# Gathering the 32-column work of a decoder step into fewer slots: when the modulation weights are asked for, and how many of their steps run together

## The chip, the core and the metric

The kernel runs on one core of a Trainium2 chip. The metric is the time of one execution in device microseconds, lower being better. Three timed runs of the kernel before lie between 1823.52 and 1826.77 us, with a median of 1824.22 us.

## The reference

One decoder layer over 256 prompt tokens and 8 sample tokens, in float32. A modulation vector is made from a conditioning input, three mixers run in parallel and are merged, and a squared-ReLU MLP follows:

```python
mod = jax.nn.silu(c) @ p['w_ada'][l] + p['b_ada'][l]
sh1, sc1, gt1, sh2, sc2, gt2 = jnp.split(mod[:, None, :], 6, axis=-1)
h = rmsnorm(x, p['g_pre_mix'][l]) * (1.0 + sc1) + sh1
z = h @ p['w_in'][l]
...
y_a = spatial_gating(...)                                  # branch A
o_hg, S_hg = gated_linear_recurrence(q_hg, k_hg, ...)      # branch B, 8 heads
o_g, S_g = gated_linear_recurrence(q_g, k_g, ...)          # branch C, 4 heads
merged = gates[:, :, 0] * (branches[0] @ p['w_branch'][l, 0])
...
x = x + gt1 * rmsnorm(merged @ p['w_out'][l], p['g_post_mix'][l])
h2 = rmsnorm(x, p['g_pre_mlp'][l]) * (1.0 + sc2) + sh2
y2 = jnp.square(jax.nn.relu(h2 @ p['w_mlp_up'][l])) @ p['w_mlp_down'][l]
x = x + gt2 * rmsnorm(y2, p['g_post_mlp'][l])
```

The samples carry states: for each of 8 sample tokens, the recurrences B and C read a state from memory, decay it, add an outer product, write it back and read it with the query.

## The kernel before

All 264 tokens stand in the columns of the moving operand and the weights are stationary. The unit of the large products is a **granule**: 512 KB of a weight matrix, that is four blocks of 128 rows by 256 columns. Each weight tile `raw` is split on the chip into a rounded high part `whi` (a cast on ScalarE, line 109) and a rest `wlo` (a subtraction on VectorE, line 106), and a granule is 24 matmuls of 128x264: `whi` with both halves of the activations and `wlo` with the first (lines 659 to 661). The loads of `raw` go through SyncE's queue, four buffers deep; `Stream.ahead` keeps two granules split ahead of TensorE. Granules are counted here from the start of the program.

Beside the large products stand small ones whose stationary operand has only 32 columns, so that four of them share the array:

- the **modulation steps**: `mod` is built 2048 columns at a time (a round), in 16 steps of 1 MB of `w_ada`. A step is four matmuls at line 376 (eight in the trace, since each is run as two). `Rounds.load` asks for its two half-tiles of 512 KB; the first step of a batch goes into `araw`, the others into tiles `b` of the common pool. `Rounds.tick` decides when, `Rounds.due` whether a batch can be run. Four rounds of 16 steps run beside the mixers and the MLP; the first two of the six parts of `mod` are made earlier, by other code (line 308).
- the **levels** (line 679): 32x32 products of the recurrences within a chunk.
- the **samples** (line 686): the queries of a sample token against its updated state `st`. A state is fetched by a DMA from GpSimd's queue, scaled on ScalarE (line 1104), given the outer product with `vbc` on VectorE (line 1106), and written back, again by GpSimd's queue. `vbc` holds value rows, repeated over the partitions by a DMA; there are two buffers of `vbc`.

`slot()` runs whatever of the three kinds waits, one after the other. `background()` is called once per granule: it advances the clock `now`, pumps the generators of the mixers, and calls `slot()` by a rule: when a batch of modulation steps is due and either a level or sample has waited or `pace` granules have passed since the last load, or when a level or sample has waited four granules.

What sets the order: TensorE's and GpSimd's instructions stand as the code is written. ScalarE's, VectorE's and SyncE's are placed by a scheduler in this part of the program, and each engine then runs its own list in order. The recurrence B runs in two groups of heads (first and second group below), C is the third group.

Of the kernel before, what the change touches and what calls it, by code (L numbers as in the profile page):

```python
# [48 lines left out]
SLOT_WAIT = 4  # L49
# [2 lines left out]
FETCHED = 3  # L52
AGE = 2
ADA_LAND = 4


@with_exitstack
def hybrid_step_kernel(
# [27 lines left out]
    def blk(shape=None, dt=F32):  # L86
        shape = shape or [P, 4, NT]
        return blkp.tile(shape, dt, tag="b", name=nm("b"))

    def sm(shape=None):  # L90
        return psm.tile(shape or [P, 512], F32, tag="sm", name=nm("sm"))
# [230 lines left out]
    class Rounds:  # L322
# [2 lines left out]

        def __init__(self):
            self.todo, self.ws, self.done, self.at = [], [], None, 0
            self.pace, self.batch = 5, 1

        def load(self, place=None):  # L330
            r, k = self.todo.pop(0)
# [18 lines left out]
        def due(self):  # L350
            if self.ws:
                return self.full() and now[0] >= self.at + ADA_LAND
            return self.done is not None and not self.todo and now[0] >= self.at + 2 * ADA_LAND

        def tick(self):
            if self.todo and not self.full() and now[0] >= self.at + self.pace:
                self.load()

        def steps(self, n=None):
# [28 lines left out]
    rounds = Rounds()  # L388

    now = [0]  # L390
# [273 lines left out]
    levels, samples = [], []  # L664

    def slot():

        lv = [x for x in levels if x[0] + AGE <= now[0]][:2]
        sv = [x for x in samples if x[0] + AGE <= now[0]]
        del levels[:len(lv)]  # L670
        del samples[:len(sv)]
        if lv:
            pl = sm([P, 2, 8, 32])
            for i, (_, lhs, rhs, _) in enumerate(lv):
                for h in range(4):
                    for hf in range(2):
                        for b in range(4):
                            t0 = hf * P + b * 32
                            T.matmul(pl[32 * b:32 * b + 32, i, 2 * h + hf, :], lhs[:, h, t0:t0 + 32], rhs[:, h, t0:t0 + 32], start=True, stop=True)  # L679
        if sv:  # L680
            G, qm, os_ = sv[0][1]
            nh = 512 // G.dv
            po = sm([P, G.dv])
            for h in range(4):
                for i, (_, _, b, sts) in enumerate(sv):
                    T.matmul(po[32 * h:32 * h + 32, :], qm[:, h, b, :], sts[h // nh][:, h % nh, :], start=i == 0, stop=i == len(sv) - 1)  # L686
        if rounds.due():
            rounds.steps()
        for i, (_, _, _, put) in enumerate(lv):
            put(pl[:, i])  # L690
        if sv:
            if sv[0][2] == 0:
                V.tensor_copy(os_, po)
            else:
                add(os_, os_, po)

    later = []

    def background():

        now[0] += 1
        while later and later[0][0] < now[0]:
            later.pop(0)[1]()
        bg.pump(rate[0])
        bs.pump(rate[1])
        wait = max([now[0] + 1 - AGE - x[0] for x in levels + samples] + [0])
        if wait and any(x[1][0].i == 2 for x in samples):
            wait += 2
        if rounds.due() and (wait or now[0] >= rounds.at + rounds.pace) or wait >= SLOT_WAIT:
            slot()  # L710
        rounds.tick()

# [3 lines left out]
    def linear(w, k0, nk, c0, width, xh, xl):  # L716

        acc = new_acc()
        kc = min(nk, 1024 // width)
        for kb in range(0, nk, kc):  # L720
            granule(w, k0, kc, c0, width, [acc], xh, xl, kb, kb == 0, kb + kc == nk)
            background()
        return acc[:, 0:width // P, 0:NT]
# [4 lines left out]
    def pair(b, g):  # L728
        return b[:, 2 * g:2 * g + 2, :]
# [9 lines left out]
    def zin(c0, width=CW):  # L739
        return linear(win, 0, KT, c0, width, hH, hL)  # L740
# [233 lines left out]
    def log_sigmoid(out, z, a):  # L974

        S.activation(a, z, AF.Abs)
        yield
        S.activation(a, a, AF.Exp, scale=-1.0)
        yield 1.6
        S.activation(a, a, AF.Ln, bias=1.0)  # L980
        yield 1.8
        V.scalar_tensor_tensor(out, z, 0.0, a, ALU.min, ALU.subtract)
        yield
# [45 lines left out]
    def gla_group():  # L1029
        G = Group()  # L1030
        G.dv, G.i = 256, 2
        G.q, G.g, G.k, G.v = blk(), blk(), blk(), [blk(), blk()]
        wl = blk([P, 512 + NT])
        wup, lr = wl[:, 0:512], wl[:, 512:512 + NT]
        nc.gpsimd.memset(wl, 0.0)
        nc.gpsimd.dma_start(wup[0:16], gla_w_up[0])
        for s in range(2):
            z = zin(6144 + s * CW)
            S.copy(pair(G.q, s), z)
        for s in range(2):  # L1040
            z = zin(6656 + s * CW)
            S.activation(pair(G.k, s), z, AF.Copy, scale=GLA_SCALE)
        z = zin(9216, P)
        S.copy(lr[0:16], z[0:16, 0, :])
        for s in range(4):
            z = zin(7168 + s * CW)
            S.copy(pair(G.v[s // 2], s % 2), z)
            ps = sm()
            T.matmul(ps[:, 0:NT], wup[:, s * P:(s + 1) * P], lr, start=True, stop=True)
            V.tensor_scalar(G.g[:, s, :], ps[:, 0:NT], bupT[:, s:s + 1], None, ALU.add)  # L1050
        G.s_in = lambda b, h, n: state_gla[0, b, h:h + n].rearrange("h k v -> k h v")
        G.s_out = lambda b, h, n: gla_sample[0, b, h:h + n].rearrange("h k v -> k h v")
        G.p_out = lambda h, n: gla_prompt[0, 0, h:h + n].rearrange("h k v -> k h v")

        def gates():
            yield from log_sigmoid(G.g, G.g, blk())
            V.tensor_scalar(G.g, G.g, 1.0 / GLA_TAU, None, ALU.mult)
            yield

        G.gates = gates  # L1060
        return G
# [246 lines left out]
    for i in range(2):  # L1308
        Gs.append(hg_group(i))
        gens.append(mixer_r(Gs[i]))  # L1310
        bg.g.append(gens[i])
    rate[:] = RATES[0]
    Gs.append(gla_group())
    gens.append(mixer_r(Gs[2]))
    bg.g.append(gens[2])
# [15 lines left out]
    def branch(n, parts):  # L1331
        for m in range(8):
            if m == 0:
                yh, yl = parts()
            z = zin(9232 + n * D + m * CW)
            gt = tmp([P, 2, NT], "gt")
            S.activation(gt, z, AF.Tanh, scale=0.5)
            pr = linear(w_branch[0, n], 0, 8, m * CW, CW, yh, yl)
            if n == 0 and m % 2 == 0:
                mg[m // 2] = blk()  # L1340
            dst = pair(mg[m // 2], m % 2)

            if n == 0:
                V.scalar_tensor_tensor(dst, gt, 1.0, pr, ALU.add, ALU.mult)
            else:
                V.scalar_tensor_tensor(gt, gt, 1.0, pr, ALU.add, ALU.mult)
                add(dst, dst, gt)
            if n == 2 and m % 2 == 1:
                a, b = blk(dt=F32R), blk(dt=F32R)
                split_tokens(mg[m // 2], a, b)  # L1350
                mh.append(a)
                ml.append(b)

    def gate_tiles(c0):

        out = [blk(), blk()]
        for s in range(4):
            z = zin(c0 + s * CW)
            gt = pair(out[s // 2], s % 2)
            S.activation(gt, z, AF.Tanh, scale=0.5)  # L1360
            V.scalar_tensor_tensor(gt, gt, 1.0, z, ALU.add, ALU.mult)
        return out
# [5 lines left out]
    def parts_b(gates):  # L1368
        for i in range(2):
            finish(i)  # L1370
            o = Gs[i].o[0]
            V.scalar_tensor_tensor(o, o, hgnT, gates[i], ALU.mult, ALU.mult)
        return yparts([Gs[0].o[0], Gs[1].o[0]])
# [16 lines left out]
    rate[:] = RATES[1]  # L1390
    branch(0, parts_a)
    gates_b = gate_tiles(5120)
    rounds.batch = 2
    branch(1, lambda: parts_b(gates_b))
    rate[:] = RATES[2]
    rounds.pace, rounds.batch = 4, 4
    gates_c = gate_tiles(8192)
    rate[:] = RATES[3]
    branch(2, lambda: parts_c(gates_c))
# [90 lines left out]
    rounds = pre  # L1490
# [112 lines left out]
    def begin_up():  # L1603

        accs = [new_acc(), new_acc()]
        for k in range(0, KT, 2):
            granule(w_mlp_up[0], 0, 2, 0, 2 * CW, accs, h2H, h2L, k, k == 0, k + 2 == KT)
            if k % 4 == 0 and k + 4 < KT:
                quad(k // 4 + 1)
            elif k + 6 < KT:  # L1610
                residual(k // 4 + 2)
            elif k + 2 == KT:
                residual(0)
            if k >= 8:
                background()
        return [a[:, :, 0:NT] for a in accs]
# [141 lines left out]
```

## Time and profile before

| | |
|---|---|
| median of three runs | 1824.22 us |
| profiled execution, its time | 1827.14 us |
| its span | 1825.4 us |
| TensorE busy | 1780.2 us (98%) |
| VectorE, ScalarE, GpSimd busy | 1181.2, 1001.2, 132.3 us |
| data moved | 442.05 MB, mean 242 GB/s |
| matmuls of lines 659 to 661 | 3 x 4624 |
| matmul records of line 376 | 296 from `araw`, 216 from `b` |

The profile comes from one execution. Matmuls are pipelined, so a busy TensorE is not TensorE at its peak: what a small product costs is read in the timeline, from the start of the last large matmul ahead of it to the start of a large matmul behind it. "PEclk" is the granted share of TensorE's clock.

### The profile page before, as it was taken

The page shows a single profiled execution, that of the slowest core. Times are in us where ns is not written, and L with a number is a line of the kernel's source. Part 1 is how long each engine was busy: PE and PEld are TensorE (multiplying, and loading weights), DVE is VectorE, ACT ScalarE, POOL GpSimd, SP SyncE. Part 2 cuts the span into 40 slices and gives each one's busy share as a digit, 9 for nine tenths or more (in the row PEclk, how much of TensorE's full clock was granted, in tenths as well). Part 3 has the DMA queues.
Part 4 walks back from the last instruction along what each step waited for, and adds up shares of the span by engine and source line. Part 5 has one row for each costly group of instructions (what it writes and reads, how often), then busy time and mean ns, then how long its engine had stood idle before and what let it go on. Part 6 is the DMA issues. An engine that isn't in the chain of part 4 may idle for free.

```text
span 1825.4 us, 42105 instructions
## 1 busy us (share of the span) xinstructions
PE 1780.2 (98%) x16964; PEld 1690.1 (93%) x16964; DVE 1181.2 (65%) x2092; ACT 1001.2 (55%) x1827; POOL 132.3 (7%) x211
## 2 busy tenths in 40 slices
PE   6999999999999999999999999999999999999998
PEld 4889999989989998989999989999999999999997
DVE  4566677787677696566555667555666666666666
ACT  5444364676766766655444666554554545454554
POOL 4221100102101111210000000000000000000000
PEclk9999999999999999999999999999999999999999
DMA  9999687688788789897988954777666666666663
GB/s 317 360 332 313 197 300 236 210 257 284 239 283 261 236 271 299 264 326 244 305 252 266 330 167 153 250 255 221 196 197 196 196 194 196 193 196 196 196 197 106
DMA packets 330179, 442.05 MB, mean 242 GB/s; under 512 B 14946, under 2 KB 276944, under 8 KB 329984
## 3 DMA queue, kind: packets, MB, share of 16 engines
q1 hardware_dynamic: 311728, 380.26, 65.1%
q0 software_dynamic: 17184, 57.85, 9.1%
q8 instruction: 133, 2.18, 0.5%
q10 hardware_dynamic: 1072, 1.25, 0.2%
q14 instruction: 62, 0.51, 0.1%
HBM read 427.60 MB, written 11.70 MB: 241 GB/s over the span
## 4 chain that ended last, share of the span: by engine, by line
PE 87%; DMA 2%; DVE 2%; issue 2%; ACT 1%; POOL 0%; DVEq 0%; ACTq 0%; POOLq 0%
PE mm L659 27%; PE mm L661 26%; PE mm L660 26%; PE ada L376 3%; DMA vbc<-vs_d 1%; PE ada L308 1%; DVE wlo L106 1%; PE sm L851 1%; DMA raw<-in_w_in_dram 1%; PE sm L679 1%; PE sm L686 0%; DVE b L106 0%; PE sm L1575 0%; DMA st<-in_state_hgrn_dram 0%; DVE b L100 0%
## 5 line engine op out<-in xcount | busy, mean ns | idle before, releaser
L659 PE MATMUL mm<-b,whi 128*128 128x264 f32 x4624 | 1292.7, 280 | 11.7 <-ACT b L825 3.6
L661 PE MATMUL mm<-b,wlo 128*128 128x264 f32 x4624 | 1279.4, 277 | 5.3 <-DVE wlo L106 5.0
L660 PE MATMUL mm<-b,whi 128*128 128x264 f32 x4624 | 1278.8, 277 | 1.9 <-issue 1.1
L106 DVE TENSOR_TENSOR wlo<-raw,whi 128x512 fp32r<-128x512 f32 x1136 | 774.5, 690 | 487.7 <-ACT whi L109 475.8
L109 ACT CAST whi<-raw 128x512 fp32r<-128x512 f32 x1136 | 691.4, 616 | 645.7 <-DVE wlo L106 332.0
L659 PEld LDWEIGHTS mm<-b,whi 128*128 128x128 f32 x4624 | 876.0, 189 | 53.9 <-issue 26.6
L661 PEld LDWEIGHTS mm<-b,wlo 128*128 128x128 f32 x4624 | 876.0, 189 | 7.1 <-DVE wlo L106 7.1
L660 PEld LDWEIGHTS mm<-b,whi 128*128 128x128 f32 x4624 | 876.3, 190 | 2.9 <-issue 1.2
L103 DVE TENSOR_TENSOR b<-b,mm 128x528 f32<-128x528 f32 (+1 forms) x137 | 95.7, 699 | 24.5 <-PE mm L661 12.9
L1106 DVE SCALAR_TENSOR_TENSOR st<-vbc,b,st 128x128 f32<-128x128 f32 (+1 forms) x96 | 34.2, 391 | 52.7 <-DMA vbc<-vs_d 47.5
L1104 ACT ACTIVATE st<-st,fs 128x128 f32<-128x128 f32 (+1 forms) x96 | 37.0, 429 | 46.3 <-DMA st<-in_state_hgrn_dram 27.8
L488 POOL DMA_DIRECT2D b<-in_w_ada_dram x64 | 46.3, 726 | 126.9 <-PE ada L308 94.4
L376 PE MATMUL ada<-araw,cT 128*32 128x512 f32 x296 | 39.8, 601 | 0.0
L308 PE MATMUL ada<-b,cT 128*32 128x256 f32 (+1 forms) x640 | 34.6, 351 | 2.7 <-DMA b<-in_w_ada_dram 2.5
L100 DVE TENSOR_TENSOR b<-b,b 128x512 f32<-128x512 f32 (+1 forms) x47 | 34.0, 744 | 1.3 <-ACT b L1218 1.0
L1107 POOL DMA_DIRECT2D out_dram<-st x32 | 23.6, 737 | 131.7 <-DVE st L1106 131.6
L308 PEld LDWEIGHTS ada<-b,cT 128*32 128x32 f32 x640 | 17.6, 112 | 14.7 <-DMA b<-in_w_ada_dram 6.3
L376 PE MATMUL ada<-b,cT 128*32 128x512 f32 x216 | 26.2, 593 | 0.0
L106 DVE TENSOR_TENSOR b<-gt,b 128x528 fp32r<-128x528 f32 x32 | 22.8, 712 | 3.2
L106 DVE TENSOR_TENSOR b<-b 128x1024 f32<-128x1024 f32 (+1 forms) x24 | 24.4, 1019 | 0.0
L1629 ACT ACTIVATE b<-vt 128x528 fp32r<-128x528 f32 x32 | 22.9, 717 | 1.0
L106 DVE TENSOR_TENSOR b<-b,b 128x1056 fp32r<-128x1056 f32 (+3 forms) x21 | 20.9, 993 | 4.0 <-ACT b L109 3.9
(343 smaller groups left out, 844.6 us busy)
## 6 DMA issues: line engine op xcount, KB each, us to landing
raw<-in_w_in_dram SPq DMA_DIRECT2D x231, 512.0 KB, 4.9
raw<-in_w_mlp_up_dram SPq DMA_DIRECT2D x128, 512.0 KB, 3.9
raw<-in_w_mlp_down_dram SPq DMA_DIRECT2D x128, 512.0 KB, 3.7
araw<-in_w_ada_dram SPq DMA_DIRECT2D x74, 512.0 KB, 5.9
b<-in_w_ada_dram SPq DMA_DIRECT2D x54, 512.0 KB, 6.6
b<-in_w_ada_dram POOLq DMA_DIRECT2D x48, 512.0 KB, 8.6
raw<-in_w_branch_dram SPq DMA_DIRECT2D x48, 512.0 KB, 4.6
raw<-in_w_out_dram SPq DMA_DIRECT2D x32, 512.0 KB, 5.4
```

The lines of the kernel that those rows point to most:

```text
L100: V.tensor_tensor(o, a, b, op=ALU.mult)
L103: V.tensor_tensor(o, a, b, op=ALU.add)
L106: V.tensor_tensor(o, a, b, op=ALU.subtract)
L109: S.copy(hi, src)
L308: T.matmul(acc[32 * j:32 * j + 32, 0:n], cT[:, k, :], w[:, n * j:n * j + n], start=k == 0, stop=k == KT - 1)
L376: T.matmul(self.acc[32 * j:32 * j + 32, :], cT[:, k, :], ws[j // 2][:, j % 2 * 512:j % 2 * 512 + 512], start=k == 0, stop=k == KT - 1)
L488: queue.dma_start(w[:, i], w1[k * P:(k + 1) * P, :, self.k0 * P:(self.k0 + self.n) * P])
L659: T.matmul(o, a, xh(k + j), start=first and j == 0, stop=False)
L660: T.matmul(o, a, xl(k + j), start=False, stop=False)
L661: T.matmul(o, b, xh(k + j), start=False, stop=last and j == n - 1)
L1104: S.activation(st[:, i, :], st[:, i, :], AF.Copy, scale=fs[:, h0 + i, b:b + 1])
L1106: V.scalar_tensor_tensor(st[:, i, :], v[:, i, :], k[:, h0 + i, NP + b:NP + b + 1], st[:, i, :], ALU.mult, ALU.add)
```

## The change

`gap` is new: while it is set (2, from the building of the third group to the end of branch B), the next modulation step is asked for two granules after the last load, if the batch is not full, in place of five. While it is set, the batch is two steps, but one as long as levels or samples stand in a queue or did within the last six granules (`QUIET`), and this last rule holds only until branch A is done (`narrow[1]`). Steps that no level or sample calls for run after `pace` times the batch, that is ten granules for a pair. With branch C's gates, `gap` goes back to 0 and the old rule holds.

```diff
@@ -52,6 +52,7 @@
+QUIET = 6
@@ class Rounds
-            self.pace, self.batch = 5, 1
+            self.pace, self.batch, self.gap = 5, 1, 0
@@ def tick
-            if self.todo and not self.full() and now[0] >= self.at + self.pace:
+            if self.todo and not self.full() and now[0] >= self.at + (self.gap or self.pace):
                 self.load()
@@
-    later = []
+    later, narrow = [], [-QUIET, True]
     def background():
+        if levels or samples:
+            narrow[0] = now[0]
+        if rounds.gap:
+            rounds.batch = 1 if narrow[1] and now[0] < narrow[0] + QUIET else 2
         now[0] += 1
...
-        if rounds.due() and (wait or now[0] >= rounds.at + rounds.pace) or wait >= SLOT_WAIT:
+        if rounds.due() and (wait or now[0] >= rounds.at + rounds.pace * (rounds.batch if rounds.gap else 1)) or wait >= SLOT_WAIT:
             slot()
         rounds.tick()
@@
     rate[:] = RATES[0]
+    rounds.gap = 2
     Gs.append(gla_group())
@@
     branch(0, parts_a)
     gates_b = gate_tiles(5120)
-    rounds.batch = 2
+    narrow[1] = False
     branch(1, lambda: parts_b(gates_b))
     rate[:] = RATES[2]
-    rounds.pace, rounds.batch = 4, 4
+    rounds.pace, rounds.batch, rounds.gap = 4, 4, 0
```

The count of instructions stays as it was, but for one addition on VectorE (line 103, the sum over samples `os`) and one modulation step that loads into `b` in place of `araw`. Six lines are added to the file, so a line number of the changed kernel is one to six higher.

Where the order changes, in three places. First TensorE: a lone modulation step of branch A's stage (granule 85), and then, in the second group (granules 153 and 154), two slots. `sm` are the levels' sums and the samples' outputs, `ada` the modulation sums, `mm` the large products. Before:

```order
L376 MATMUL ada_3266<-araw_3736,cT 32x512 x2
L376 MATMUL ada_3266<-araw_3738,cT 32x512 x2
...
L679 MATMUL sm_7431<-b_7097 32x32 x32
L679 MATMUL sm_7431<-b_7173 32x32 x32
L686 MATMUL sm_7496<-st_7041,b_7039 32x128 x4
...
L679 MATMUL sm_7544<-b_7290 32x32 x32
L376 MATMUL ada_7049<-araw_7292,cT 32x512 x2
L376 MATMUL ada_7049<-araw_7294,cT 32x512 x2
```

Now, at granule 92 and at granule 158:

```order
L377 MATMUL ada_3266<-araw_3736,cT 32x512 x2
L377 MATMUL ada_3266<-araw_3738,cT 32x512 x2
L377 MATMUL ada_3266<-b_3976,cT 32x512 x2
L377 MATMUL ada_3266<-b_3978,cT 32x512 x2
...
L680 MATMUL sm_7771<-b_7426 32x32 x32
L680 MATMUL sm_7771<-b_7635 32x32 x32
L687 MATMUL sm_7836<-st_7262,b_7007 32x128 x4
L377 MATMUL ada_7099<-araw_7594,cT 32x512 x2
L377 MATMUL ada_7099<-araw_7596,cT 32x512 x2
```

The lone step has become a pair, and the slot with two levels and a sample now takes a modulation step along. Counting the unbroken runs of 32-column products behind the code of line 308, there are 52 before and 44 now. By stage: granules 80 to 108, five and two; first group (109 to 135), eight and seven; between the groups, two and one; second group (149 to 175), nine and seven; third group (184 to 230), twelve and thirteen; then four batches of four and two. The rest is the same.

Second SyncE's queue in the third group, at the load of the 222nd to 227th granule. `raw` are granules of the stream, `araw` and `b` halves of a modulation step. Before:

```order
L616 DMA raw_10724<-in_w_in_dram 128x4x256
L339 DMA b_11163<-in_w_ada_dram 128x1024
L339 DMA b_11165<-in_w_ada_dram 128x1024
L616 DMA raw_10782<-in_w_in_dram 128x4x256
L339 DMA araw_10746<-in_w_ada_dram 128x1024
L339 DMA araw_10748<-in_w_ada_dram 128x1024
L339 DMA b_11320<-in_w_ada_dram 128x1024
L616 DMA raw_10829<-in_w_in_dram 128x4x256
L339 DMA b_11322<-in_w_ada_dram 128x1024
L616 DMA raw_10863<-in_w_in_dram 128x4x256
L616 DMA raw_10905<-in_w_branch_dram 128x4x256
L616 DMA raw_10939<-in_w_branch_dram 128x4x256
```

Now:

```order
L340 DMA b_10846<-in_w_ada_dram 128x1024
L340 DMA b_10848<-in_w_ada_dram 128x1024
L617 DMA raw_10882<-in_w_in_dram 128x4x256
L340 DMA b_11096<-in_w_ada_dram 128x1024
L617 DMA raw_10921<-in_w_in_dram 128x4x256
L340 DMA b_11098<-in_w_ada_dram 128x1024
L617 DMA raw_10958<-in_w_branch_dram 128x4x256
L340 DMA b_11439<-in_w_ada_dram 128x1024
L617 DMA raw_10992<-in_w_branch_dram 128x4x256
L340 DMA b_11441<-in_w_ada_dram 128x1024
L340 DMA araw_11008<-in_w_ada_dram 128x1024
L340 DMA araw_11010<-in_w_ada_dram 128x1024
```

Between the same granules there are eight halves now, after two more just ahead of these rows, and six before. From the 182nd to the 227th granule in SyncE's queue there are 32 halves now and 24 before; a place with four halves and at most one `raw` between them stands new at the 215th.

Third VectorE at the first three sample states of the first group. `wlo` rows are the halves of a granule's split, `st` rows the outer products of a state, one for each head. Before:

```order
L1106 SCALAR_TENSOR_TENSOR st_4978<-vbc_5147,b_4774,st_4978 128x128
L1106 SCALAR_TENSOR_TENSOR st_5071<-vbc_5308,b_4774,st_5071 128x128 x2
L106 TENSOR_TENSOR wlo_5098<-raw_4970,whi_5097 128x512
L1106 SCALAR_TENSOR_TENSOR st_5071<-vbc_5308,b_4774,st_5071 128x128 x2
L106 TENSOR_TENSOR wlo_5102<-raw_4970,whi_5101 128x512
L106 TENSOR_TENSOR wlo_5136<-raw_5020,whi_5135 128x512
L1106 SCALAR_TENSOR_TENSOR st_5306<-vbc_5393,b_4774,st_5306 128x128 x3
```

Now:

```order
L1111 SCALAR_TENSOR_TENSOR st_4978<-vbc_5143,b_4770,st_4978 128x128 x3
L107 TENSOR_TENSOR wlo_4963<-raw_4840,whi_4962 128x512
L1111 SCALAR_TENSOR_TENSOR st_5067<-vbc_5306,b_4770,st_5067 128x128 x4
L107 TENSOR_TENSOR wlo_4967<-raw_4840,whi_4966 128x512
L107 TENSOR_TENSOR wlo_5005<-raw_4887,whi_5004 128x512
L1055 TENSOR_SCALAR b_3857<-sm_5025,vec 128x264
L107 TENSOR_TENSOR wlo_5009<-raw_4887,whi_5008 128x512
L107 TENSOR_TENSOR b_5103<-b_176 128x4x256
L107 TENSOR_TENSOR wlo_5054<-raw_4923,whi_5053 128x512
L1111 SCALAR_TENSOR_TENSOR st_5304<-vbc_5393,b_4770,st_5304 128x128
```

The third state's first product stood three halves (1.5 granules) behind the first state's last one and stands five halves (2.5 granules) behind it now, and the first two states stand some three granules earlier. On ScalarE the fourth state's scaling stands 1.5 granules behind the first state's last product on VectorE, now as before.

## The prediction

> **What bounds the kernel now.** I read the page first: the busy shares, then the chain that ended last.
>
> ```profile
> span 1825.4 us, 42105 instructions
> PE 1780.2 (98%) x16964; PEld 1690.1 (93%) x16964; DVE 1181.2 (65%) x2092; ACT 1001.2 (55%) x1827; POOL 132.3 (7%) x211
> PE 87%; DMA 2%; DVE 2%; issue 2%; ACT 1%; POOL 0%; DVEq 0%; ACTq 0%; POOLq 0%
> ```
>
> TensorE carries 87% of the chain. A slot is on the path for as long as it keeps the large matmuls from starting, and what else the chain holds are stalls in which they wait for an operand. So two things have to be priced: slots, and stalls that the moved loads make or unmake. For the slots I read TensorE's timeline, whose first column is the start. First the steady beat with a pair of modulation steps behind it, then a lone step.
>
> ```profile
> 1144.68 0.28 PE L660 MATMUL mm<-b,whi 128*128 128x264 f32 x1
> ...
> 1145.47 0.28 PE L661 MATMUL mm<-b,wlo 128*128 128x264 f32 x1
> 1145.67 1.06 PE L376 MATMUL ada<-araw,cT 128*32 128x512 f32 x8
> 1146.56 1.04 PE L376 MATMUL ada<-b,cT 128*32 128x512 f32 x8
> ...
> 1147.74 0.28 PE L660 MATMUL mm<-b,whi 128*128 128x264 f32 x1
> ...
> 310.96 0.28 PE L661 MATMUL mm<-b,wlo 128*128 128x264 f32 x1
> 311.17 1.07 PE L376 MATMUL ada<-araw,cT 128*32 128x512 f32 x8
> ...
> 312.38 0.28 PE L660 MATMUL mm<-b,whi 128*128 128x264 f32 x1
> ```
>
> Seven large matmuls start within 0.79 us, so the beat is 0.113 us and a granule of 24 takes 2.7 us. The first large matmul behind a slot starts late by the second as well, so I measure up to the second one and take off two beats (0.23 us). A lone step costs 312.38 - 310.96 - 0.23 = 1.19 us, a pair 1147.74 - 1145.47 - 0.23 = 2.04 us. Two lone steps cost 2.38 us: **0.34 us** of a slot is fixed, for going to 32 columns and back, and 0.85 us is the step. The same for a sample in the third group, alone and with a pair behind it:
>
> ```profile
> 804.71 0.28 PE L661 MATMUL mm<-b,wlo 128*128 128x264 f32 x1
> 804.91 0.64 PE L686 MATMUL sm<-st,b 128*32 128x256 f32 x8
> ...
> 805.70 0.28 PE L660 MATMUL mm<-b,whi 128*128 128x264 f32 x1
> ...
> 722.66 0.28 PE L661 MATMUL mm<-b,wlo 128*128 128x264 f32 x1
> 722.87 0.64 PE L686 MATMUL sm<-st,b 128*32 128x256 f32 x8
> 723.33 1.04 PE L376 MATMUL ada<-araw,cT 128*32 128x512 f32 x8
> 724.18 1.04 PE L376 MATMUL ada<-b,cT 128*32 128x512 f32 x8
> ...
> 725.37 0.28 PE L660 MATMUL mm<-b,whi 128*128 128x264 f32 x1
> ```
>
> Alone it costs 0.76 us, with the pair 2.48 us; apart the two would cost 0.76 + 2.04 = 2.80 us. Riding along saves 0.32 us. I take 0.33 us for a slot that goes.
>
> Then the stalls, by the waits. The first two rows are of the first group (383 to 406 us), the next three of the third group's end (780 to 806 us), the last of a smaller stall (712 to 720 us); columns are total, count and longest wait in us.
>
> ```profile
> ACT st L1104 <- DMA st<-in_state_hgrn_dram: 9.2, 1, 9.2
> DVE st L1106 <- DMA vbc<-vs_d: 6.2, 1, 6.2
> ...
> ACT whi L109 <- DMA raw<-in_w_in_dram: 7.6, 2, 4.1
> PE mm L661 <- DVE wlo L106: 2.6, 1, 2.6
> DVE st L1106 <- issue: 4.0, 1, 4.0
> ...
> ACT whi L109 <- DMA raw<-in_w_in_dram: 2.4, 1, 2.4
> ```
>
> In the first group the splits of the large products stand behind a sample's operation that waits for its DMA; in the third group behind late `raw` tiles as well. How much the DMA engines move there shows in windows of the stages (the last columns are TensorE's clock, DMA share, GB/s):
>
> ```profile
> 672.00:720.00 48.00, 45.17 (x575) 42.12 (x573) 36.69 (x65) 31.45 (x65) 8.00 (x12) 1.00 0.87 287
> 720.00:765.00 45.00, 44.93 (x367) 41.12 (x365) 23.60 (x49) 28.29 (x66) 9.47 (x14) 1.00 0.83 265
> 765.00:800.00 35.00, 33.01 (x297) 29.90 (x295) 18.50 (x35) 18.03 (x36) 9.28 (x14) 1.00 1.00 365
> ```
>
> Until 765 us there is room. From 765 to 800 us the engines are full, at 365 GB/s.
>
> **The change part by part.**
>
> *Fewer slots.* Eight unbroken runs of 32-column products go, out of 52. No product goes, so each saves only the fixed part: 8 x 0.33 = **2.6 us**, all of it on the path, since TensorE is what ends last between the stalls. It takes lone steps in the first 108 granules (three slots), steps that now ride with samples in both groups of branch B and between them (four), two of the four late batches, and gives one slot back in the third group.
>
> *The added sum on VectorE.* Here is its row, for the groups of branch B:
>
> ```profile
> L103 DVE TENSOR_TENSOR os<-os,sm 128x128 f32<-128x128 f32 x7 | 2.0, 281 | 0.4 <-PE sm L686 0.3
> ```
>
> One more of 0.28 us, on an engine busy 65% of the span: nothing, and 0.3 us if it fell where VectorE is behind.
>
> *Earlier loads.* Between the 182nd and 227th granule in SyncE's queue stand 8 more halves of 512 KB, that is 4.2 MB: the last steps come before the third group's end instead of after it. A half of a lone step was asked for some granules after its `araw` had been read; now it is asked for in the same call that runs the slot, so its DMA waits in SyncE's queue for TensorE, and `raw` loads stand behind it. That queue is about seven granules ahead of TensorE (four `raw` buffers and three split granules), or 19 us, so such a wait alone reaches nothing. What can reach TensorE is a burst. Here is what one cost before, by the longest piece of the chain and TensorE's first matmul after it:
>
> ```profile
> 701.22 11.56 DMA raw<-in_w_in_dram
> 715.50 0.38 PE L659 MATMUL mm<-b,whi 128*128 128x264 f32 x1 [0.78 <-ACT gt L1337]
> ```
>
> SyncE had issued four halves from 695.85 to 699.82 us with one `raw` among them, and the next `raw` took 11.56 us to land. ScalarE waited 2.4 us for it and TensorE 0.78 us. One such place of four halves is new (at the 215th granule), the others were there in some form. So the lower bound is 0, for a burst that the 265 GB/s of its stage leaves room for, and the upper one is its 2.1 MB at 365 GB/s, 5.7 us, if nothing hid it. I take **+0.8 us**, the row of the nearest burst. At the end (765 to 800 us) the burst grows by two halves, 1.05 MB, in a stage without room: 2.9 us more of transfers at 365 GB/s. TensorE was released at 800.58 us by `wlo`, behind a state's operation that waited until then, with `raw` late at the same time; the row is below. I take 0 for it, since the state's wait holds the same matmul anyway, and keep 2.9 us for the range.
>
> *Moved states.* The fetches keep their order on GpSimd's queue, and their distances on VectorE and ScalarE stay near what they were, but for the first group. I take 0 and price it as a rival.
>
> The sum: -2.6 + 0.8 = **-1.8 us**. The profiled execution took 1827.14 us, 1.7 us more than its span and 2.9 us more than the median of 1824.22 us; taken off the span it makes 1823.6 us, and against the median **1822.4 us**.
>
> **The rivals.** What a stall costs beyond its own length shows at the third group's end:
>
> ```profile
> 797.73 0.28 PE L660 MATMUL mm<-b,whi 128*128 128x264 f32 x1
> 800.58 0.38 PE L661 MATMUL mm<-b,wlo 128*128 128x264 f32 x1 [2.57 <-DVE wlo L106]
> ...
> 801.53 0.43 PE L661 MATMUL mm<-b,wlo 128*128 128x264 f32 x1
> 801.75 0.43 PE L659 MATMUL mm<-b,whi 128*128 128x264 f32 x1
> ...
> 804.39 0.37 PE L659 MATMUL mm<-b,whi 128*128 128x264 f32 x1
> ```
>
> The gap costs 2.85 - 0.11 = 2.74 us, and from 801.53 to 804.39 us matmuls start every 0.22 us, at half the beat: 13 of them take 2.86 us in place of 1.47 us, **1.4 us** more. The Trainium skill (TensorE: Matmul & The Clock Gate, What's actually happening) puts the clock down after an idle window of about 3.4 us; here 2.57 us of idleness was enough. By the page's rule the 1.4 us would not be paid for a new gap of that length.
>
> *Slower: the third group starves.* The new burst and the longer one make a stall of their own, of the kind just shown, at another place: 2.74 + 1.4 us, and the old one grows by 2.9 us: -2.6 + 7.0 = +4.4 us, 1828.6 us. For it speaks a stage at 365 GB/s that gets a tenth more; against it that 720 to 765 us had 265 GB/s. It decides when ScalarE's wait for a `raw` tile passes the 4.1 us of before. The Trainium skill (DMA: Bandwidth & Descriptors, Specifications) has about 358 GB/s from memory for one core; the 365 GB/s here exceed that, and by the page the last stage's 12.8 + 1.05 MB would take 38.7 us in place of 35, 3.7 us more rather than 2.9. It speaks for this rival.
>
> *Faster: the first group's stall goes.* TensorE's gaps there:
>
> ```profile
> 397.97 0.28 PE L661 MATMUL mm<-b,wlo 128*128 128x264 f32 x1
> 399.87 0.38 PE L659 MATMUL mm<-b,whi 128*128 128x264 f32 x1 [1.62 <-ACT whi L109]
> 400.08 0.28 PE L660 MATMUL mm<-b,whi 128*128 128x264 f32 x1
> 401.04 0.38 PE L661 MATMUL mm<-b,wlo 128*128 128x264 f32 x1 [0.68 <-DVE wlo L106]
> ```
>
> That is 1.8 + 0.85 us, and half the beat after it for another 1.4 us: 4.0 us. The third state's products now stand 2.5 granules behind the first's (6.8 us) in place of 1.5 (4.1 us), more nearly what the 6.2 us wait asks for. If all of it went: -1.8 - 4.0 = -5.8 us, 1818.4 us. Against it: ScalarE's wait of 9.2 us on the fourth state came first, and there the distance stays 1.5 granules.
>
> *No gain: the fixed part is not saved.* If the switch hides elsewhere, say because a slot's work only makes TensorE wait less for a split, +0.8 us is left: 1825.0 us. The three prices above that agree (0.34, 0.32) speak against it.
>
> **How the numbers follow.** About 0.2% (3.65 us) is what a measurement of this kernel tells from no change. The forecast has 47%, the slower rival 25%, the faster 20%, no gain 8%. Faster by over 0.2% (under 1820.6 us): 0.20 from the faster rival and 0.07 from the forecast, where part of that stall goes: 0.27. Slower by over 0.2% (over 1827.9 us): 0.25. Within: 0.48. The range takes in both rivals, 1818.4 and 1828.6 us, and a little at either end, since each could come with the bound of another term: 1817.0 to 1829.5 us.
>
> **What would show it.** Right: lone steps in branch A's stage as pairs of 2.04 us; a slot with two levels, a sample and a step without a second slot within four granules; two late batches of four in place of four. Slots summed alone should be 2.6 us shorter. Wrong: ScalarE's waits for `raw` in the third group over 10 us in all, or half the beat at a place where the clock was full before, or a first group without a gap over 1 us.

## The result: half a per cent slower

Five runs of the changed kernel have a median of 1835.08 us (1832.72 to 1837.24), five of the kernel before beside them 1826.73 us (1823.52 to 1827.27). The ratio is 1.0044, with a 95% interval from 1.0034 to 1.0055: 8 us slower, outside the range of 1817.0 to 1829.5 us. Its profiled execution has a span of 1830.9 us, 5.5 us more than before; it is the fastest of its five runs, and the profiled one of before is slower than its median, so these two traces show 5.5 of the 8 us. The page:

```profile
span 1830.9 us, 42103 instructions
PE 1781.1 (97%) x16964; PEld 1692.2 (92%) x16964; DVE 1180.2 (64%) x2093; ACT 1003.2 (55%) x1827; POOL 132.0 (7%) x211
```

TensorE's busy time grew by 0.9 us only, so the time went into gaps. I took every start of a large matmul between 240 and 1400 us in both traces, subtracted the beat, and sorted what was left. Small products and the fixed parts of their slots: 149.3 us before, 146.4 us after, **2.9 us less**. Stalls: 18.8 and 27.5 us, **8.7 us more**. Half the beat: 4.5 and 4.6 us. The sum, +5.9 us, is the 5.5 us of the spans within what such sorting can do. Where a slot also holds a stall, its own part is an estimate from the undisturbed slots. Their price holds: in the kernel before, the 35 slots between 200 and 1400 us that hold only steps, levels and samples and no stall, fitted by what they contain, have a fixed part of 0.33 us.

The two largest new gaps, in TensorE's timeline of the changed kernel:

```profile
451.16 0.28 PE L662 MATMUL mm<-b,wlo 128*128 128x264 f32 x1
451.36 0.66 PE L687 MATMUL sm<-st,b 128*32 128x128 f32 x16
451.82 1.23 PE L377 MATMUL ada<-araw,cT 128*32 128x512 f32 x8
456.05 0.58 PE L660 MATMUL mm<-b,whi 128*128 128x264 f32 x1 [2.99 <-ACT gt L1343]
456.42 0.43 PE L661 MATMUL mm<-b,whi 128*128 128x264 f32 x1
...
778.78 0.28 PE L662 MATMUL mm<-b,wlo 128*128 128x264 f32 x1
782.39 0.65 PE L1296 MATMUL sm<-cst,b 128*128 128x128 f32 x4 [3.33 <-ACT b L1298]
```

Less the small products between them they are stalls of 3.4 and 3.6 us, and behind the first the large matmuls start every 0.22 us, half the beat (the granted clock is 0.60 from 455.5 to 458.5 us and 1.00 from 440 to 450 us). Both times TensorE waits for ScalarE. What held ScalarE is in the waits of the whole span, kernel before first, changed kernel second (total us, times, longest):

```profile
DVE st L1106 <- DMA vbc<-vs_d: 47.5, 19, 6.8
ACT st L1104 <- DMA st<-in_state_hgrn_dram: 27.8, 8, 9.2
ACT st L1104 <- DMA st<-in_state_gla_dram: 12.6, 7, 3.2
ACT st L1104 <- PE mm L661: 5.9, 1, 5.9
DVE st L1106 <- issue: 5.2, 2, 4.0
```

```profile
DVE st L1111 <- DMA vbc<-vs_d: 49.7, 20, 6.7
ACT st L1109 <- DMA st<-in_state_gla_dram: 33.3, 11, 7.0
ACT st L1109 <- DMA st<-in_state_hgrn_dram: 21.5, 7, 5.4
DVE st L1111 <- issue: 13.3, 3, 6.3
ACT st L1109 <- PE sm L1296: 5.3, 1, 5.3
ACT b L1221 <- DVE st L1111: 4.5, 1, 4.5
```

The waits ahead of the samples' state operations grew from 46.3 to 60.1 us on ScalarE and from 52.7 to 63.0 us on VectorE; in the trace of the change's second measurement they are 65.3 us on each. Both engines run their lists in order, so the splits of the large products wait behind them. At 456 us it was ScalarE's operation of line 1221 that waited 4.5 us for a state's sum on VectorE, which had waited 2.2 us for its values. How this looks at 782 us, in the changed kernel's timeline (GpSimd, SyncE, ScalarE):

```profile
770.73 0.72 POOL L1083 DMA_DIRECT2D st<-in_state_gla_dram  x1 [14.98 <-PE sm L687]
771.45 0.57 POOL L1089 DMA_DIRECT2D vbc<-vs_d  x1
...
771.32 0.81 SPq L340 DMA_DIRECT2D araw<-in_w_ada_dram  x2
...
777.27 0.91 ACT L1109 ACTIVATE st<-st,fs 128x256 f32<-128x256 f32 x2 [5.33 <-PE sm L1296]
778.08 1.12 ACT L110 CAST whi<-raw 128x512 fp32r<-128x512 f32 x2
781.36 0.51 ACT L1109 ACTIVATE st<-st,fs 128x256 f32<-128x256 f32 x1 [2.16 <-DMA st<-in_state_gla_dram]
781.77 1.54 ACT L1298 COPY b<-sm 128x512 f32<-128x512 f32 x3
```

One slot frees the buffer of a state and that of a modulation step. GpSimd asks for the next state at 770.73 us, SyncE for two halves of weights at 771.32 us. ScalarE stands still from 771.94 to 777.27 us at the state's scaling; the profile names the products of line 1296 there, which had ended at 776.35 us. The state's own load, issued at 770.73 us, took 6.5 us to land, that is until the scaling starts: this is what it waited for. Two splits, and ScalarE waits again, with the copy that TensorE wants (line 1298) behind it.

### The profile page after: what moved, and what is told of

It is laid out like the page before. It is cut to its first block, busy times and chain, and to the rows that moved or that the text cites. A ratio compares the mean times of both kernels' runs of the same rounds, so it can differ in the third digit from the quotient of the medians.

```text
span 1830.9 us, 42103 instructions
## 1 busy us (share of the span) xinstructions
PE 1781.1 (97%) x16964; PEld 1692.2 (92%) x16964; DVE 1180.2 (64%) x2093; ACT 1003.2 (55%) x1827; POOL 132.0 (7%) x211
## 2 busy tenths in 40 slices
DMA packets 330179, 442.05 MB, mean 241 GB/s; under 512 B 14946, under 2 KB 276944, under 8 KB 329984
## 4 chain that ended last, share of the span: by engine, by line
PE 86%; issue 3%; DVE 2%; DMA 2%; ACT 1%; POOL 0%; SPq 0%; DVEq 0%; ACTq 0%; POOLq 0%
PE mm L660 26%; PE mm L662 26%; PE mm L661 26%; PE ada L377 3%; PE ada L309 1%; DVE wlo L107 1%; DMA araw<-in_w_ada_dram 1%; PE sm L856 1%; DMA vbc<-vs_d 1%; PE sm L680 1%; DMA st<-in_state_gla_dram 0%; PE sm L687 0%; PE sm L1581 0%; DMA st<-in_state_hgrn_dram 0%; DVE b L104 0%
## 5 line engine op out<-in xcount | busy, mean ns | idle before, releaser
L660 PEld LDWEIGHTS mm<-b,whi 128*128 128x128 f32 x4624 | 876.0, 189 | 51.2 <-issue 20.2
L1111 DVE SCALAR_TENSOR_TENSOR st<-vbc,b,st 128x128 f32<-128x128 f32 (+1 forms) x96 | 33.8, 392 | 63.0 <-DMA vbc<-vs_d 49.7
```

What stands on the lines that cost most here:

```text
L660: T.matmul(o, a, xh(k + j), start=first and j == 0, stop=False)
L1111: V.scalar_tensor_tensor(st[:, i, :], v[:, i, :], k[:, h0 + i, NP + b:NP + b + 1], st[:, i, :], ALU.mult, ALU.add)
```

## The experiments

Theory A: the places of the state operations in the two queues cause it. Theory B: the weights, loaded earlier, crowd the DMA engines and the `raw` tiles come late. The first four runs led to theory C: the weights make the *states'* loads late, and the states block the splits. Ratios are to the kernel before, run on the same chip, with their 95% intervals; the change's own is 1.0044. Differences within a pair are those of its two ratios times 1827 us.

**Without the steps' loads.** In both kernels:

```diff
+            if not place and self.kept:
+                self.ws.append((r, k, self.kept))
+                self.at = now[0]
+                return
             for i in range(2):
```

> The changed kernel without its loads of modulation weights in the background steps: the first pair of halves that lands is kept and every later step multiplies with it (so the steps' weights are wrong and 2 MB of traffic for each step is left out). Slots, their order and the places of the samples' states stay. Theory A (a sample's state operations stand too close, in ScalarE's and VectorE's in-order queues, behind the slot and the loads that feed them): the added stalls do not come from these loads, so this kernel stays 5 to 8 us above the kernel before with the same loads left out, and the stalls near 456 and 782 us stay, each over 2 us. Theory B (the loads, moved earlier, crowd the DMA engines): the stalls go, and this kernel is 2 to 3 us below its partner, the price of eight slots.

> The kernel before, with the same loads of modulation weights left out. It is the partner to subtract: theory A has it 5 to 8 us faster than the changed kernel without these loads, theory B 2 to 3 us slower. Against the kernel before itself: theory A 1824 to 1827 us, theory B the same or up to 4 us less.

The changed kernel so cut ran at 0.9962 (0.9947 to 0.9977; 1817.25 us), its partner at 0.9968 (0.9957 to 0.9979; 1820.33 us). The 8 us are gone: theory A alone falls, since the state operations stood where they had, or within a granule and a half of it. Whether the slots' 2.6 us came through here this pair does not tell: the changed kernel is 1.1 us below its partner by the ratios and 3.1 us by the medians. The waits ahead of state operations fell with the weights, to 49.3 us on ScalarE and 47.4 us on VectorE in the changed kernel (partner: 45.3 and 46.7 us). But `raw` was not late in the changed kernel either. From 680 to 830 us ScalarE waited for it like this, before and then after:

```profile
ACT whi L109 <- DMA raw<-in_w_in_dram: 10.0, 3, 4.1
ACT whi L109 <- DMA raw<-in_w_branch_dram: 4.5, 2, 4.1
```

```profile
ACT whi L110 <- DMA raw<-in_w_in_dram: 4.8, 3, 2.3
```

**Without the states' loads.** One state tile and one value tile are loaded in each group, and reused:

```diff
-            nc.gpsimd.dma_start(st, G.s_in(b, h, nh))
+            if not kept:
+                kept.append(tmp([P, 4, P], "vbc", VB_BUFS).rearrange("p (h j) v -> p h (j v)", h=nh))
+                nc.gpsimd.dma_start(kept[0], G.s_in(b, h, nh))
...
-                S.activation(st[:, i, :], st[:, i, :], AF.Copy, scale=fs[:, h0 + i, b:b + 1])
+                S.activation(st[:, i, :], kept[0][:, i, :], AF.Copy, scale=fs[:, h0 + i, b:b + 1])
```

> The changed kernel without the loads of the samples' states and values: in each group of samples one state tile and one value tile are loaded once, and every sample scales and adds these (so the samples' results are wrong, and their loads are left out). Slots, ScalarE's, VectorE's and TensorE's work, the write-backs of the states and all modulation weights stay. Theory A: a state's scaling no longer waits for a fetch that waits for a slot, so the stalls behind it go: 1819 to 1824 us, and against the kernel before with the same loads left out -3 to +1 us. Theory B: the modulation weights still crowd the large products' tiles, so the difference to the partner stays at +4 us or more.

> The kernel before, with the same loads of states and values left out. It is the partner to subtract. Theory A: 1819 to 1824 us, its own stalls behind states (about 10 us of its 15) go as well, and eight more slots (2.6 us) are what sets it above the changed kernel. Theory B: at least 4 us below the changed kernel with the same loads left out.

0.9928 (0.9913 to 0.9942) and 0.9924 (0.9910 to 0.9939): 21 us less for the changed kernel, 14 us less for the kernel before, and no difference that can be told between them. Both are below the 1819 us that theory A expected at least: the states cost more than it had them at. All the weights are still loaded where the change puts them, and the loss is gone, which speaks against theory B. Two things weaken this cut: it also leaves out 15.2 of 442.05 MB, and the state operations stand earlier in it, on VectorE by up to 10.5 granules. With `raw` no later (the rows above), theory B falls. The loss needs both kinds of loads.

**Half the weights, and the same weights later.** In the first, `ws.append(ws[0])` replaces the load of the second half; in the second the loads go through `later`, two granules on.

> The changed kernel, in which a background step loads only the first of its two halves of modulation weights and uses it twice (the steps' results are wrong; half of their traffic, 1 of every 2 halves of 512 KB, is left out). Slots, states and everything else stay. The first four runs showed that the added time needs both the weight loads and the state loads. Theory C (joint: a state's loads share the DMA engines with the weights and land later, at places where the splits stand close behind the state): about half of the gain of leaving out all of them, so 1824 to 1829 us. Theory A alone (places of the state operations only): 1833 us or more.

> The changed kernel, with each background load of modulation weights put two granules later in SyncE's queue (5.4 us); slots keep their places, and so do the states of the second and third group, while the first group's early states move by a granule. Theory C1 (the moment: weights are asked for as the very slot ends that lets GpSimd ask for the next state, so that the two collide): 1826 to 1831 us, the stall near 783 us under 1.5 us. Theory C2 (the amount in the stage: about as many loads in it, wherever in a period they stand): 1833 to 1838 us, that stall stays over 2.5 us.

Half the weights: 1.0001 (0.9986 to 1.0016; 1827.28 us), half-way between all (1835 us) and none (1817 us), as theory C has it. Two granules later: 1.0028 (1.0014 to 1.0043; 1832.41 us), between the two expectations and overlapping the interval of the change itself; its stall near 782 us was still 4.2 us long. So the moment of asking is not shown to matter. In the third group the amount had grown, too. Issues from 680 to 830 us (count, size, median us to landing), before and then after:

```profile
araw<-in_w_ada_dram SPq DMA_DIRECT2D x8, 512.0 KB, 8.0
vbc<-vs_d POOLq DMA_DIRECT2D x13, 256.0 KB, 5.9
st<-in_state_gla_dram POOLq DMA_DIRECT2D x12, 256.0 KB, 5.8
```

```profile
araw<-in_w_ada_dram SPq DMA_DIRECT2D x14, 512.0 KB, 8.6
vbc<-vs_d POOLq DMA_DIRECT2D x13, 256.0 KB, 7.4
st<-in_state_gla_dram POOLq DMA_DIRECT2D x12, 256.0 KB, 6.5
```

Six more halves through `araw`, and a value tile lands 1.5 us later, a state 0.7 us. The Trainium skill (DMA: Bandwidth & Descriptors, Issuing engines are not separate DMA queues) says that loads run on the same 16 DMA engines and interleave, whichever engine issues them; these rows agree.

**One part of the program each.** `rounds.gap, rounds.batch = 0, 2` at the end of branch A's stage ends the new rule there; `rounds.gap = 2` moved to that place begins it there.

> The new rule up to the end of branch A's stage, that is with the first two groups of samples, and the rule of before in the third group (45 slots). Slots: 7 x 0.33 us less than before. If the loss is the third group's (its stalls grew by about 3.5 us), this is 1827 to 1829 us; if the first group's (4 us), 1828 to 1831 us. If each stage pays its own part, this and the next kernel add up to the change: their two differences to the kernel before make +8 us.

> The rule of before up to the third group of samples, the new one there (52 slots, as before: no slot is saved in this part). Groups one and two as in the kernel before, so their stalls should be those of before. Third group alone: its stalls grow by about 3.5 us, so 1829 to 1831 us. If this comes out within 1.5 us of the kernel before, the third group's new stalls are only moved from elsewhere.

Up to branch A's end: 1.0011 (0.9998 to 1.0024; 1831.01 us), 2 us slower although seven slots are gone, with no change still inside the interval. From there on: 1.0031 (1.0019 to 1.0043; 1832.93 us), 5.7 us slower with no slot saved, more than the 1829 to 1831 us expected. Within their intervals they add up to the change's 8 us. By these ratios the larger part is the third group's.

**The state work on another engine.** The scaling alone:

```diff
-                S.activation(st[:, i, :], st[:, i, :], AF.Copy, scale=fs[:, h0 + i, b:b + 1])
+                nc.gpsimd.tensor_scalar(st[:, i, :], st[:, i, :], fs[:, h0 + i, b:b + 1], None, ALU.mult)
```

In `after_pool` and `before_pool` the outer product and the sum are moved as well, as two further GpSimd instructions.

> The changed kernel with the samples' state operations (the scaling of the state, its outer product and the sum) on GpSimd instead of ScalarE and VectorE; slots, fetches and weight loads keep their places. No split of the large products stands behind a state's operation any more. Theory C (weights and state loads share the DMA engines, and the late state blocks the splits queued behind its operations): the stalls behind states go although all the traffic stays: 1815 to 1823 us, and under the kernel before with the same move. If late raw tiles are what stops the splits (theory B), the stalls stay: 1830 us or more. If GpSimd is too slow for the states, slots wait for them and new stalls show with a sample's product as their releaser.

> The kernel before with its state operations moved to GpSimd in the same way: the partner. Theory C: its own stalls behind states go too, 1815 to 1823 us, and 1 to 3 us more than the changed kernel so moved, for its eight further slots. Theory B: no nearer than 5 us to the changed kernel so moved, and below it.

> The changed kernel with only the scaling of the state on GpSimd; the outer product and sum stay on VectorE. ScalarE's splits are then free of states, VectorE's are not. Theory C: part of the gain of moving both, as VectorE still waited 50 us in all for the values' loads: 1820 to 1830 us. If ScalarE's wait for the fetch is the only one that counts, the same as with both moved.

All of it on GpSimd did not give the 1815 to 1823 us of theory C: 1.0131 (1.0112 to 1.0150) and 1.0144 (1.0129 to 1.0160), 24 and 26 us slower than the kernel before. What was expected if GpSimd is too slow came true: in the changed kernel so moved slots wait for the states (from 380 to 830 us):

```profile
PE sm L687 <- POOL st L1112: 16.1, 11, 5.9
```

The scaling alone is the run that tells most: **0.9963** (0.9950 to 0.9976; 1820.50 us), 15 us under the changed kernel, with every load kept and every slot at its granule. ScalarE waits for no state any more, and VectorE 14.0 us for values where it had waited 49.7 us:

```profile
DVE st L1111 <- POOL st L1109: 23.4, 23, 2.6
DVE st L1111 <- DMA vbc<-vs_d: 14.0, 5, 3.0
```

In the third group the stall near 782 us is gone: from 680 to 800 us no idle time of TensorE over 0.5 us is left. The first group's is not. There VectorE still waits for values, with TensorE behind it (VectorE's row, then TensorE's):

```profile
452.09 0.61 DVE L1111 SCALAR_TENSOR_TENSOR st<-vbc,b,st 128x128 f32<-128x128 f32 x2 [2.98 <-DMA vbc<-vs_d]
...
453.36 1.30 PE L1234 MATMUL sm<-b,b 128*128 128x128 f32 x8 [2.33 <-DVE b L101]
...
457.11 1.11 PE L1241 MATMUL sm<-cst,b 128*128 128x128 f32 x4 [1.59 <-DVE os L104]
```

So ScalarE's in-order wait for states is shown as the cause in the third group. In the first group the late values on VectorE are read from the traces alone, and this run also moved that group's outer products by up to 7.5 granules.

**Partner, further buffers, and the change once more.** `after_pool1_vb` has four buffers of `vbc` and 27 instead of 28 of the common pool, and asks for values a state earlier.

> The kernel before with only the scaling of the states on GpSimd: the partner of the changed kernel so moved, which ran at 0.9963 of the kernel before. If the change lost its slots' gain only to states that block ScalarE's splits, the partner is 1 to 3 us above 1820.5 us (52 slots in place of 44). If the new rule still costs elsewhere (longer unbroken runs that wait for instructions, as the runs without state loads suggest with a gain of nothing), the two are within 1 us, or the partner is lower.

> The changed kernel with the scaling on GpSimd and with two more buffers for the values' tiles (one buffer of the general pool less), the values asked for one state earlier. The third group's samples then follow each other faster (the last at the 219th granule instead of the 228th), with 44 slots. Theory C: VectorE's waits for the values' loads (some 14 us left from the 380th to the 830th us) go, and 1 to 4 us of stalls with them: 1816 to 1820 us. If samples that follow faster crowd the DMA engines more, 1820 us or more.

> The changed kernel itself, on the chip of these runs, so that it stands beside the others: 1.0034 to 1.0055 of the kernel before, as at first.

The change again: 1.0040 (1.0020 to 1.0061). The partner: **0.9960** (0.9945 to 0.9975; 1819.18 us), no different from the changed kernel so moved. Each is about 7 us below the kernel before and 15 us below the changed one: without states on ScalarE the new rule costs nothing that can be told, and adds nothing. The further buffers lost, at 1.0074 (1.0059 to 1.0089; 1840.35 us where 1816 to 1820 us were expected). The longest gap there, 8.4 us of stall, is a wait of TensorE for VectorE in the second group, whose samples that edit moved as well; it tells nothing of the values alone.

**Neither kind of load.** With both kinds of loads left out, the slots are what is left of the change.

> The changed kernel without the background steps' loads of modulation weights and without the loads of states and values (one tile of each is kept and reused, so mod and the samples' results are wrong). What is left of the change is the 44 slots in place of 52, the further sum and the moved instructions. The slots' term alone: 2 to 3 us less than the partner, near 1809 us. If waits for instructions in the longer unbroken runs eat it: within 1 us of the partner.

> The kernel before, with both kinds of loads left out in the same way: the partner. 1811 us, 2 to 3 us more than the changed kernel so cut, if a slot's fixed part of 0.33 us is saved eight times and nothing takes its place.

0.9922 (0.9906 to 0.9937) and 0.9915 (0.9901 to 0.9929): the 2.6 us are not in the time. Nor are they in the four pairs taken together: from its partner the changed kernel stands -1.1 us (no weights), +0.7 (no states), +0.5 (scaling on GpSimd) and +1.3 (neither load), on average +0.4 us, give or take 1.8 us if the pairs count as independent. They do show in the timeline: sorted as above, small products and slots take 149.1 us in the partner and 146.1 us in the changed kernel, 3.1 us less. But stalls take 6.6 and 11.2 us, and none of the further ones is behind a load. The two largest, first the changed kernel so cut, then the partner at the same work of the second group:

```profile
325.00 0.39 PE L245 MATMUL sm<-vsb,cst 128*128 128x8 f32 x2 [0.56 <-DVE vsb L104]
...
540.29 0.97 PE L688 MATMUL sm<-b 128*32 128x32 f32 x89
...
541.10 0.69 PE L695 MATMUL sm<-st,b 128*32 128x128 f32 x15
541.52 1.02 PE L385 MATMUL ada<-araw,cT 128*32 128x512 f32 x3
544.30 1.06 PE L385 MATMUL ada<-araw,cT 128*32 128x512 f32 x5 [1.76 <-issue]
```

```profile
536.80 0.89 PE L687 MATMUL sm<-b 128*32 128x32 f32 x82
...
537.55 0.41 PE L694 MATMUL sm<-st,b 128*32 128x128 f32 x6
...
541.09 0.72 PE L687 MATMUL sm<-b 128*32 128x32 f32 x62 [0.24 <-DVE b L100]
541.63 0.60 PE L384 MATMUL ada<-araw,cT 128*32 128x512 f32 x1
```

A level is 64 products in the trace. The partner runs two levels and one sample state, then large matmuls, then one level and the step. The changed kernel runs two levels (128 products), 16 products of the samples and eight of the step without a break, and stops 1.76 us in the middle of the step while nothing that the profile shows is awaited. The stall is 2.75 us in all. At 325 us a lone step had stood in the partner; it now rides in a pair elsewhere, and a product of branch A waits for VectorE: 0.85 us. In this pair the gathered slots lose at these places what they save.

The length of the run alone does not make the stop. In the same trace a run of the same make-up, in the first group, goes through:

```profile
418.52 1.26 PE L688 MATMUL sm<-b 128*32 128x32 f32 x126
...
420.05 1.12 PE L385 MATMUL ada<-araw,cT 128*32 128x512 f32 x8
421.10 0.38 PE L668 MATMUL mm<-b,whi 128*128 128x264 f32 x1
```

The run of the second group stops for 0.7 to 1.9 us in nine traces that have this order, and not in that of `after_pool`; the first group's has no such stop in any of them. The kernel before shows a stop of 2.1 us without a releaser as well, in a run of 64 products near 675 us. What TensorE waits for there stays open.

## Why the prediction was wrong, point by point

- **Fewer slots, -2.6 us.** The mechanism and the price were right (-2.9 us in the full kernels' timelines, -3.1 us without loads), but not that all of it stays on the path. The first step that failed is "all of it on the path, since TensorE is what ends last between the stalls". One of the longer runs brought a stall without a releaser (2.75 us without loads), and a step's absence uncovered a wait for VectorE (0.85 us). The rival "no gain" had this outcome, by another way than the one it named.
- **The added sum, 0.** Nothing speaks against it: the row of `os` in the groups of branch B went from seven operations and 2.0 us to eight and 2.3 us.
- **Earlier loads, +0.8 us.** Mis-sized, and put on the wrong tile. I priced bursts by ScalarE's wait for `raw`, which fell from 14.5 to 4.8 us in the third group. The same traffic came out in the states' waits there: ScalarE 15.3 to 35.5 us, VectorE 20.2 to 35.2 us, all rows of state operations from 680 to 830 us together.
- **Moved states, 0.** This is the step that cost the 8 us: "their distances on VectorE and ScalarE stay near what they were, but for the first group. I take 0". The forecast priced this term as a rival in the faster direction only. Counted in the traces, ScalarE's scaling in the third group stands on average 3.3 granules behind the slot that frees its buffer, where it had been 3.7 (the first of the two states of each slot), and the state's load lands 0.7 us later, the values' 1.5 us. In place of 0, the waits ahead of state operations grew by 13.8 us on ScalarE and 10.3 us on VectorE in the whole span, and with the scaling off ScalarE the 8 us are gone. In the first group the last state stands 2.0 granules behind the product that frees its values on VectorE, where it had been 5.0; there the 3.4 us at 456 us arose. The rows of before had shown the waits' size (46 and 53 us ahead of state operations) and that the splits stand behind them. They should have been the first thing priced, and with the load counted in.
- **The rivals.** "The third group starves" had the sign, the stage and the weights; its price was +4.4 us and the runs gave +8 us, since the states are late sooner than `raw` and the first group pays too. Its mark, a wait for `raw` of over 10 us, did not come; half the beat at new places did. "The first group's stall goes" did not happen: 3.4 us from 386 to 401 us became 3.3 us from 387 to 393 us, and 456 us came on top.

What stays open: what TensorE waits for in the stop of the second group (the page of the profile lists a DMA queue of instructions, so late instructions are a guess and no more); how the third group's loss divides between the amount of traffic and the shorter distance, as no run changes only the distance; and what the late values of the first group cost by themselves.

## What to carry to other kernels

Before moving loads, list what waits longest on an in-order engine that also feeds the critical one, and price the change by what it does to those waits; here a late 256 KB tile with splits queued behind it cost more than a late 512 KB tile with buffers ahead of it. When a stall needs two causes, cut each alone and then both in the old and the new kernel: only the pairs told here that a saving was in the timeline and not in the time. And an operation whose operand comes late may be better off on an engine with nothing urgent behind it, even where it runs at half the speed. There is a limit to it: the scaling on GpSimd gained, the scaling with the outer product and the sum lost.

## What the runs showed of the hardware

GpSimd scales a state more slowly than ScalarE, and VectorE's operations on the states become slower meanwhile. Groups by line and form, in the changed kernel and with the scaling on GpSimd (busy us, mean ns, then idle time):

```profile
L1109 ACT ACTIVATE st<-st,fs 128x128 f32<-128x128 f32 x64 | 21.5, 391 | 21.8 <-DMA st<-in_state_hgrn_dram 21.5
L1111 DVE SCALAR_TENSOR_TENSOR st<-vbc,b,st 128x128 f32<-128x128 f32 x64 | 19.4, 347 | 25.1 <-DMA vbc<-vs_d 25.1
```

```profile
L1109 POOL TENSOR_SCALAR st<-st,fs 128x128 f32<-128x128 f32 x64 | 52.3, 829 | 20.3 <-ACT fs L1074 19.8
L1111 DVE SCALAR_TENSOR_TENSOR st<-vbc,b,st 128x128 f32<-128x128 f32 x64 | 24.8, 400 | 21.8 <-POOL st L1109 11.3 <-issue 4.7 <-DMA vbc<-vs_d 3.0
```

829 ns for 391 ns, and 400 ns for 347 ns; the kernel still gained 15 us. The Trainium skill (GPSIMD Engine Reference, Specifications) has GpSimd and VectorE share their interface to SBUF, with contention where a VectorE instruction reads two inputs there; the second pair of rows agrees. I had also not expected that one run of 152 products of 32 columns stops for 0.7 to 1.9 us without a releaser in nine traces, while another of the same make-up never does.
